# Strassen operand sums of two feed-forward layers moved from VectorE to GpSimd

## The chip, the cores and the metric

The kernel runs on one core of one Trainium2 chip. The metric is the device time of one execution in microseconds, as the median of several runs. TensorE (PE) does the matrix products, VectorE (DVE) and ScalarE (ACT) the elementwise work, GpSimd (POOL) masks and small fills. A product's result goes to a bank of PSUM, everything else lies in SBUF.

## What is computed

One layer of a hybrid decoder trunk on 1024 tokens of width 1024, in float32, cut here to what the change touches:

```python
def swiglu(h, w_gate, w_up, w_down):
    a = jnp.einsum("bld,df->blf", h, w_gate)
    b = jnp.einsum("bld,df->blf", h, w_up)
    return jnp.einsum("blf,fd->bld", jax.nn.silu(a) * b, w_down)

x = x + 0.5 * swiglu(rms_norm(x, ffn1_norm), ffn1_w_gate, ffn1_w_up, ffn1_w_down)   # D_FF = 2816
x = x + hybrid_mixer(rms_norm(x, mix_norm), ...)      # gated delta rule heads and Mamba2 heads
x = x + 0.5 * swiglu(rms_norm(x, ffn2_norm), ffn2_w_gate, ffn2_w_up, ffn2_w_down)
return rms_norm(x, final_norm)
```

## The kernel before

**Precision.** A float32 operand is split into two tiles, hi and lo. `split2` does it: ScalarE casts the operand to hi (L239), VectorE subtracts hi from the operand and so gets lo (L240). A product of weights `a` and tokens `b` is then three matmuls for each of 4 blocks of the contraction: hi by hi (L332), hi by lo (L333), lo by hi (L334), 12 in all, into a bank of 128x512. In the trace the parts are called `ah`, `al`, `bh`, `bl`.

**Strassen.** Gate and up projections multiply 2x2 blocks in seven products instead of eight. Product 1 takes `r11 + r22` of the tokens and `a11 + a22` of the weights, product 5 `r22` and `a11 + a12`, product 7 the token block (0, k + 4) plus `r22` and `a12 - a22`. The operands of the first weight tiles of gate and up are made ahead of the main loop. `b_first` and `b_second` make the token operands: TensorE transposes a block of tokens into a PSUM bank (L216), VectorE scales it by the norm's weights and adds or subtracts the other block (L279), or for product 1 adds two blocks in SBUF (L294). `a_start(n)` makes the weight operands, four or two at a time, by `a_ops`: a sum of two 128x512 pieces (L315), then the split. The table `A_START` says which: entry 2 has products 5 and 7 for gate and up (four sums), entry 3 has product 1 for gate and up (two sums).

**What stands in which order.** The code calls, in `b_second`, `between(0)` (which runs the first products through `first_products` and then `a_start` 2), then the splits of `r22`, then four operands of product 7 (k = 0 to 3), then `between(1)` (`a_start` 3), then four operands of product 1. A scheduler then sets the order of each engine's queue, and an engine works its queue strictly in that order. `gate_up_all` follows: product 6, product 5, product 7 and product 1 of the first two tiles, then the other 20 tiles one after the other in a fixed pattern. The results of the first products, of 6 and of 7 are copied out of their banks by ScalarE (L341), which frees the bank.

**Buffers.** Each of these operands is first made in a buffer of tag `q`, of which there are 4. Two of them are held by `m3`, the copies of product 3, until L400 in `gate_up_all`. So the four weight sums, four operands of product 7, two more weight sums and four token sums, 14 operands in this order, go through two buffers in turn: an operand is made when the L240 subtraction of the operand two places ahead of it has read its buffer. The banks of tag `sc`, into which the transposes write, are two as well: the transposes for k = 2 and k = 3 of product 7 write banks that L279 for k = 0 and k = 1 must have read.

Of the kernel before, what the change touches and what calls it, by code (L numbers as in the profile page):

```python
# [16 lines left out]
ALU = mybir.AluOpType  # L17
# [27 lines left out]
def kernel(  # L45
# [7 lines left out]
    V, A, G, T = nc.vector, nc.scalar, nc.gpsimd, nc.tensor  # L53
# [158 lines left out]
    def transposed(xns, k):  # L212

        pt = psum("sc")
        for i in range(4):
            T.transpose(pt[:, i * P:(i + 1) * P], xns[i][:, k * P:(k + 1) * P], ident)  # L216
        return pt
# [20 lines left out]
    def split2(hi, lo, src):  # L238
        return (A.copy(out=hi, in_=src),  # L239
                V.tensor_tensor(out=lo, in0=src, in1=hi.bitcast(F32), op=ALU.subtract))  # L240

    def split(hi, lo, src):
        return split2(hi, lo, src)[1]
# [9 lines left out]
    def b_op(H, m):  # L253
        if m not in H:
            pool, th, tl = B_TAGS[m]
            pool = pool or hbp[0]
            H[m] = (pool.tile([P, 4, 512], F32R, name=f"bh{m}", tag=th),
                    pool.tile([P, 4, 512], F32R, name=f"bl{m}", tag=tl))
        return H[m]
# [11 lines left out]
    def b_second(pool, x0, x1, wcol, H, r11, r22, between):  # L271

        def operand(m, k, f):
            t = pool.tile([P, 512], F32, name="bs", tag="q")
            f(t)
            return split2(b_op(H, m)[0][:, k], b_op(H, m)[1][:, k], t)

        def scaled(pt, kx, other, op):
            return lambda t: V.scalar_tensor_tensor(out=t, in0=pt, scalar=wcol[:, kx:kx + 1], in1=other,  # L279
                                                    op0=ALU.mult, op1=op)  # L280

        for k in range(4):
            A.mul(out=r22[:, k], in_=transposed(x1, k + 4), mul=wcol[:, k + 4:k + 5])
            p12 = transposed(x1, k)
            operand(3, k, scaled(p12, k, r22[:, k], ALU.subtract))
            operand(6, k, scaled(p12, k, r11[:, k], ALU.add))
        between(0)
        for k in range(4):
            split(b_op(H, 5)[0][:, k], b_op(H, 5)[1][:, k], r22[:, k])
        for k in range(4):  # L290
            operand(7, k, scaled(transposed(x0, k + 4), k + 4, r22[:, k], ALU.add))
        between(1)
        for k in range(4):
            last = operand(1, k, lambda t: V.tensor_tensor(out=t, in0=r11[:, k], in1=r22[:, k], op=ALU.add))  # L294
        return last

    A_GROUPS = ((3, 2, 1, 5), (4, 7, 6))
# [3 lines left out]
        nc.sync.dma_start(out=raw, in_=w.rearrange("(k p) c -> p k c", p=P)[:, :, p * 256:(p + 1) * 256])  # L301
        return raw

    def a_ops(pool, *prods):

        hi = wp.tile([P, 4, 4, P], F32R, name="ah", tag="whi")
        lo = wp.tile([P, 4, 4, P], F32R, name="al", tag="wlo")
        for i, (raw, m, ops) in enumerate(prods):
            a11, a12 = raw[:, 0:4, 0:P], raw[:, 4:8, 0:P]
            a21, a22 = raw[:, 0:4, P:2 * P], raw[:, 4:8, P:2 * P]  # L310
            v = {3: a11, 4: a22, 2: (a21, a22, ALU.add), 1: (a11, a22, ALU.add), 5: (a11, a12, ALU.add),
                 7: (a12, a22, ALU.subtract), 6: (a21, a11, ALU.subtract)}[m]
            if isinstance(v, tuple):
                t = pool.tile([P, 4, P], F32, name="as", tag="q")
                V.tensor_tensor(out=t, in0=v[0], in1=v[1], op=v[2])  # L315
                v = t
            last = split2(hi[:, i], lo[:, i], v)
            ops[m] = hi[:, i], lo[:, i]
        return last


    A_START = (((0, 2), (0, 4), (1, 2), (1, 4)), ((0, 3), (1, 3), (0, 6), (1, 6)),
               ((0, 5), (1, 5), (0, 7), (1, 7)), ((0, 1), (1, 1)))

    def a_start(pool, raws, ops, n):
        a_ops(pool, *((raws[j], m, ops[j]) for j, m in A_START[n]))

    def prod(H, bank, ops, m, first):
        (wh, wl), (bh, bl) = ops[m], H[m]
# [357 lines left out]
    with ExitStack() as c1:  # L687
        npool = NormPool(ffn_pools(c1))
        H = {}
        with tc.tile_pool(name="x1", bufs=1, side="right", reuse_waits="tile") as xp, \  # L690
# [5 lines left out]
            raws = [a_load(ffn1_w_gate[0], 0), a_load(ffn1_w_up[0], 0)]  # L696
            for b in range(4, NB):
                nc.sync.dma_start(out=xt[b], in_=x_v[:, b])
            ops = [{}, {}]
            x0, last = normalise_pairs(npool, xt, "h6")  # L700
            with tc.issue_after(last.ins), tc.issue_after(cols_in.ins):
                a_start(npool, raws, ops, 0)
            r11, r22 = (kp.tile([P, 4, 512], F32, name=f"keepx{i}") for i in range(2))
            with tc.issue_after(last_t.ins):
# [3 lines left out]
            last = b_second(npool, x0, x1, nrm[0], H, r11, r22,  # L708
                     start_rest(npool, H, ffn1_w_gate[0], ffn1_w_up[0], raws, ops))
# [100 lines left out]
    with tc.tile_pool(name="gtmp", bufs=1, side="right", reuse_waits="tile") as tp:  # L810
# [23 lines left out]
        for b in range(NB):  # L834
# [12 lines left out]
                        in1=bias.unsqueeze(1).to_broadcast([P, NB, NG]), op=ALU.add)  # L847
# [11 lines left out]
        for c in (15, 13, 11, 9, 7, 5, 3):  # L859
# [8 lines left out]
                               in1=alog.unsqueeze(1).to_broadcast([P, NB, NG]),  # L868
# [11 lines left out]
                        op=ALU.subtract)  # L880
# [19 lines left out]
    for un in range(4):  # L900
# [37 lines left out]
        for b0 in range(0, NB, 2):  # L938
# [6 lines left out]
            for name, lst, sc in (("xdt", xdts, bc2(dtn, b0)), ("xe", xes, bc2(dxe, b0))):  # L945
                t = s1.tile([P, 2, 256], F32, name=name, tag=name, bufs=4)
                last_x = V.tensor_tensor(out=t.rearrange("p i (h c) -> p i h c", h=4), in0=ptv, in1=sc,
                                         op=ALU.mult)
# [42 lines left out]
        for b0 in range(0, NB, 4):  # L991
# [33 lines left out]
            for b, py, *_ in pairs:  # L1025
                for j in range(2):
                    xv = xst[j][:, b * P:(b + 2) * P]
                    V.scalar_tensor_tensor(out=xv, in0=xv, scalar=dcol[:, 2 * un + j:2 * un + j + 1],
                                           in1=py[:, j * 256:(j + 1) * 256], op0=ALU.mult, op1=ALU.add)
# [71 lines left out]
    with ExitStack() as cg:  # L1101
        g1 = cg.enter_context(tc.tile_pool(name="gdn1", bufs=1, reuse_waits="tile"))
        g2 = cg.enter_context(tc.tile_pool(name="gdn2", bufs=2, reuse_waits="tile"))
        for h in range(GH):
# [33 lines left out]
            for half in range(2):  # L1138
# [4 lines left out]
                for i in range(4):  # L1143
# [6 lines left out]
                                in1=wend[:, hb, h:h + 1].to_broadcast([P, 4, P]), op=ALU.mult)  # L1150
# [3 lines left out]
            for b0 in range(0, NB, 2):  # L1154
# [7 lines left out]
                for i in range(2):  # L1162
# [4 lines left out]
                                in0=pg.rearrange("p (i c) -> p i c", i=2)[:, :, P:2 * P],  # L1167
                                in1=dt[:, b2], op=ALU.mult)
# [24 lines left out]
            for half in range(2):  # L1193
                pt = psum("mx")
                for i in range(4):
# [4 lines left out]
                                in1=rin[:, hb].unsqueeze(2).to_broadcast([P, 4, P]), op=ALU.mult)  # L1200
# [12 lines left out]
            for j in range(31):  # L1213
                r, n = j // 4 + 1, 31 - j
                t = ft[:, 0:r * n].rearrange("p (s l) -> p s l", l=n)
                V.tensor_tensor(out=t, in0=fx[:, 0:r, j:j + 1].to_broadcast([P, r, n]),
                                in1=fu[:, j:j + 1, j + 1:32].to_broadcast([P, r, n]), op=ALU.mult)
# [51 lines left out]
            for b in range(NB):  # L1269
                bs = slice(b * P, (b + 1) * P)  # L1270
                rr = vr[:, b]
                if st is not None:
# [4 lines left out]
                                           in1=vr[:, b], op0=ALU.mult, op1=ALU.add)  # L1277
# [8 lines left out]
                if b < NB - 1:  # L1286
# [5 lines left out]
                    else:  # L1292
                        V.scalar_tensor_tensor(out=sn, in0=st, scalar=egt[:, b, h:h + 1],
                                               in1=p3[:, 0:P], op0=ALU.mult, op1=ALU.add)
# [100 lines left out]
    raws = [a_load(ffn2_w_gate[0], 0), a_load(ffn2_w_up[0], 0)]  # L1395
    ops = [{}, {}]
# [3 lines left out]
    for b in range(NB):  # L1400
# [3 lines left out]
        if b == 5:  # L1404
            x0 = normalise(0, npool, xt2, jtag="h6")
            r11, r22 = (natp.tile([P, 4, 512], F32, name="keepx", tag=t) for t in ("nat", "zg"))
            b_first(npool, x0, nrm[2], H, r11)
    x1 = normalise(1, npool, xt2, jtag="h7")
    last = b_second(npool, x0, x1, nrm[2], H, r11, r22, start_rest(npool, H, ffn2_w_gate[0], ffn2_w_up[0], raws, ops))
    c2.close()  # L1410
    cn.close()
# [24 lines left out]
    def between():  # L1436

        with tc.issue_after(dn.last.ins):
            for b in range(4):
                V.scalar_tensor_tensor(out=xt2[b], in0=xt2[b], scalar=rows[1][:, b:b + 1], in1=rows[0],  # L1440
                                       op0=ALU.mult, op1=ALU.mult)
                nc.sync.dma_start(out=out_v[:, b], in_=xt2[b])
            for i in range(4):
                part(i, 1)
            V.tensor_scalar(out=ss[:, 4:8], in0=ss[:, 4:8], scalar1=1.0 / D, scalar2=EPS,
                            op0=ALU.mult, op1=ALU.add)
# [39 lines left out]
```

## Time and profile before

| what | value |
| --- | --- |
| median of 3 runs (lowest to highest) | 2311.04 us (2310.92 to 2312.38) |
| the profiled execution: its own time, its span | 2311.93 us, 2310.2 us |
| granted TensorE clock over the span | 0.999 |
| busy: PE, DVE, ACT, POOL | 99%, 74%, 48%, 2% |

The profile is one execution. Its span runs from the first to the last instruction; the time of the execution holds 1.7 us more. "Busy" is the share of the span in which an engine had an instruction under way. The clock is the mean of what TensorE was granted, 1 being its full speed.

### The profile page before, as it was taken

To read this page: it belongs to the slowest core of one execution; us is meant where nothing else is said; L and a number is where in the kernel's file an instruction comes from. 1 tells how busy PE (TensorE), PEld (TensorE's weight loads), DVE (VectorE), ACT (ScalarE), POOL (GpSimd) and SP (SyncE) were. 2 spreads that over 40 slices of the span, in tenths; PEclk is the share of its full clock that TensorE was granted. 3 is DMA by queue.
4 is the path that set the end of the run, shared out by engine and by line. 5 is a ranking of instruction groups with operands and counts; after the bars stand their busy time and mean duration, and the time that the engine had idled before them with its cause. 6 is when DMAs were issued, how large, how long until landed. Compare 5 with 4: busy or idle time off the path is not lost.

```text
span 2310.2 us, 31439 instructions
## 1 busy us (share of the span) xinstructions
PE 2278.0 (99%) x11766; PEld 1869.7 (81%) x11766; DVE 1701.6 (74%) x3149; ACT 1118.0 (48%) x2120; POOL 52.0 (2%) x125
## 2 busy tenths in 40 slices
PE   7999999999999999999999999999999999999998
PEld 5788888888878888887888888888878888888886
DVE  8977776767765675667778777778698777766777
ACT  7433333343467785864655456532543333334334
POOL 0000000000000000000000000000000000000000
PEclk9999999999999999999999999999999999999999
DMA  3333232574652322222333222335223333329455
GB/s 111 131 111 106 100 114 91 178 278 128 227 177 75 92 92 73 73 87 74 83 101 83 72 77 64 119 99 192 92 81 117 109 104 105 108 89 351 140 156 214
DMA packets 220956, 281.33 MB, mean 122 GB/s; under 512 B 47008, under 2 KB 153564, under 8 KB 219780
## 3 DMA queue, kind: packets, MB, share of 16 engines
q1 hardware_dynamic: 220548, 279.23, 37.2%
q8 instruction: 92, 1.51, 0.3%
q14 instruction: 60, 0.49, 0.1%
q0 software_dynamic: 256, 0.10, 0.0%
HBM read 211.55 MB, written 67.73 MB: 121 GB/s over the span
## 4 chain that ended last, share of the span: by engine, by line
PE 86%; DVE 7%; ACT 3%; DMA 2%; issue 1%; POOL 0%; SPq 0%; DVEq 0%; ACTq 0%
PE ps_pj L121 10%; PE ps_pj L122 10%; PE ps_pj L123 10%; PE ps_pj L332 6%; PE ps_pj L334 6%; PE ps_pj L333 6%; PE ps_mx L332 3%; PE ps_mx L334 3%; PE ps_mx L333 3%; PE ps_pj L553 2%; PE ps_pj L554 2%; PE ps_pj L552 2%; PE ps_oo L334 2%; PE ps_oo L332 2%; PE ps_oo L333 2%
## 5 line engine op out<-in xcount | busy, mean ns | idle before, releaser
L121 PE MATMUL ps_pj<-hhi,whi 128*128 128x512 f32 x832 | 333.9, 401 | 0.4 <-ACT gsb L826 0.4
L123 PE MATMUL ps_pj<-hhi,wlo 128*128 128x512 f32 x832 | 333.3, 401 | 0.0
L122 PE MATMUL ps_pj<-hlo,whi 128*128 128x512 f32 x832 | 332.7, 400 | 0.0
L334 PE MATMUL ps_pj<-bh,al 128*128 128x512 f32 x688 | 267.9, 389 | 0.0
L333 PE MATMUL ps_pj<-bl,ah 128*128 128x512 f32 x688 | 267.8, 389 | 0.0
L332 PE MATMUL ps_pj<-bh,ah 128*128 128x512 f32 x688 | 267.6, 390 | 0.0
L123 PEld LDWEIGHTS ps_pj<-hhi,wlo 128*128 128x128 f32 x832 | 157.1, 189 | 29.4 <-issue 0.7
L121 PEld LDWEIGHTS ps_pj<-hhi,whi 128*128 128x128 f32 x832 | 157.2, 189 | 29.0 <-ACT gsb L826 0.8
L122 PEld LDWEIGHTS ps_pj<-hlo,whi 128*128 128x128 f32 x832 | 157.0, 189 | 28.0
L239 ACT CAST ah<-wst 128x512 fp32r<-128x512 f32 x88 | 54.6, 622 | 223.1 <-PE ps_oo L333 125.3
L333 PEld LDWEIGHTS ps_pj<-bl,ah 128*128 128x128 f32 x688 | 129.2, 188 | 26.8
L334 PEld LDWEIGHTS ps_pj<-bh,al 128*128 128x128 f32 x688 | 129.1, 188 | 26.8
L332 PEld LDWEIGHTS ps_pj<-bh,ah 128*128 128x128 f32 x688 | 128.9, 188 | 26.5
L239 ACT CAST hid<-hraw 128x1024 fp32r<-128x1024 f32 (+1 forms) x84 | 82.3, 981 | 140.2 <-PE ps_oo L554 60.1
L315 DVE TENSOR_TENSOR as<-wst 128x512 f32<-128x512 f32 x220 | 145.0, 684 | 2.0 <-DMA wst<-in_ffn_w_up_dram 1.7
L240 DVE TENSOR_TENSOR al<-as,ah 128x512 fp32r<-128x512 f32 x220 | 140.9, 685 | 5.0 <-ACT ah L239 4.3
L332 PE MATMUL ps_mx<-bh,ah 128*128 128x512 f32 x352 | 138.3, 395 | 4.0 <-ACT m L341 1.4
L333 PE MATMUL ps_mx<-bl,ah 128*128 128x512 f32 x352 | 138.2, 393 | 0.5 <-DVE bl L240 0.5
L334 PE MATMUL ps_mx<-bh,al 128*128 128x512 f32 x352 | 137.5, 391 | 0.3 <-DVE al L240 0.3
L239 ACT CAST ah<-as 128x512 fp32r<-128x512 f32 x220 | 125.0, 617 | 22.6 <-DVE as L315 22.6
L240 DVE TENSOR_TENSOR hid<-hraw,hid 128x1024 fp32r<-128x1024 f32 (+1 forms) x84 | 95.0, 1131 | 31.6 <-ACT hid L239 31.0
L137 DVE TENSOR_TENSOR wlo<-wst,whi 128x1024 fp32r<-128x1024 f32 x64 | 77.5, 1218 | 48.6 <-ACT whi L136 30.5
(448 smaller groups left out, 5085.0 us busy)
## 6 DMA issues: line engine op xcount, KB each, us to landing
hraw<-hid_scr SPq DMA_DIRECT2D x70, 512.0 KB, 4.3
hid_scr<-hs SPq DMA_DIRECT2D x110, 256.0 KB, 2.3
wst<-in_ffn_w_down_dram SPq DMA_DIRECT2D x50, 512.0 KB, 4.7
wst<-in_ffn_w_gate_dram SPq DMA_DIRECT2D x22, 1024.0 KB, 5.6
wst<-in_ffn_w_up_dram SPq DMA_DIRECT2D x22, 1024.0 KB, 5.4
wst<-in_w_in_dram SPq DMA_DIRECT2D x36, 512.0 KB, 5.3
hid_scr<-sg SPq DMA_DIRECT2D x44, 256.0 KB, 2.0
keep<-in_ffn_w_down_dram SPq DMA_DIRECT2D x20, 512.0 KB, 6.4
```

Source lines behind the costliest of these rows:

```text
L121: T.matmul(o, lhsT=wh, rhs=mh, start=first, stop=False)
L122: T.matmul(o, lhsT=wh, rhs=ml, start=False, stop=False)
L123: T.matmul(o, lhsT=wl, rhs=mh, start=False, stop=last)
L137: V.tensor_tensor(out=lo[sl], in0=st[sl], in1=hi[sl].bitcast(F32), op=ALU.subtract)
L239: return (A.copy(out=hi, in_=src), V.tensor_tensor(out=lo, in0=src, in1=hi.bitcast(F32), op=ALU.subtract))
L240: V.tensor_tensor(out=lo, in0=src, in1=hi.bitcast(F32), op=ALU.subtract))
L315: V.tensor_tensor(out=t, in0=v[0], in1=v[1], op=v[2])
L332: T.matmul(bank, lhsT=wh[:, k], rhs=bh[:, k], start=a, stop=False, skip_group_check=True)
L333: T.matmul(bank, lhsT=wh[:, k], rhs=bl[:, k], start=False, stop=False, skip_group_check=True)
L334: T.matmul(bank, lhsT=wl[:, k], rhs=bh[:, k], start=False, stop=z, skip_group_check=True)
L552: T.matmul(bank, lhsT=hh, rhs=wh, start=first and k == 0, stop=False, skip_group_check=True)
L553: T.matmul(bank, lhsT=hh, rhs=wl, start=False, stop=False, skip_group_check=True)
```

## The change

Twenty sums change their engine: in each of the two feed-forward layers the four weight sums of `a_start` 2, the two of `a_start` 3, and the four token sums of product 1. What they read, where they write and who splits them stays. `G` is GpSimd, `V` VectorE.

```diff
@@ b_second @@
         for k in range(4):
-            last = operand(1, k, lambda t: V.tensor_tensor(out=t, in0=r11[:, k], in1=r22[:, k], op=ALU.add))
+            last = operand(1, k, lambda t: G.tensor_tensor(out=t, in0=r11[:, k], in1=r22[:, k], op=ALU.add))
@@ a_ops, a_start @@
-    def a_ops(pool, *prods):
+    def a_ops(pool, *prods, eng=None):
...
-                V.tensor_tensor(out=t, in0=v[0], in1=v[1], op=v[2])
+                (eng or V).tensor_tensor(out=t, in0=v[0], in1=v[1], op=v[2])
...
-        a_ops(pool, *((raws[j], m, ops[j]) for j, m in A_START[n]))
+        a_ops(pool, *((raws[j], m, ops[j]) for j, m in A_START[n]), eng=G if n > 1 else V)
```

The scheduler then orders the queues anew. First GpSimd's queue in the first feed-forward layer, behind the loads of the small columns (`as` is a weight sum, `wst` the raw weights, `bs` a token sum, `keepx0` and `keepx1` are `r11` and `r22`):

```order
 L102 DMA colst2_207<-in_ffn2_norm_dram 8x128
+L315 TENSOR_TENSOR as_559<-wst_220 128x512
+L315 TENSOR_TENSOR as_563<-wst_222 128x512
+L315 TENSOR_TENSOR as_567<-wst_220 128x512
+L315 TENSOR_TENSOR as_571<-wst_222 128x512
+L315 TENSOR_TENSOR as_625<-wst_220 128x512
+L315 TENSOR_TENSOR as_629<-wst_222 128x512
+L294 TENSOR_TENSOR bs_637<-keepx0_281,keepx1_282 128x512
+L294 TENSOR_TENSOR bs_643<-keepx0_281,keepx1_282 128x512
+L294 TENSOR_TENSOR bs_647<-keepx0_281,keepx1_282 128x512
+L294 TENSOR_TENSOR bs_651<-keepx0_281,keepx1_282 128x512
 L776 MEMSET pre_5412 128x3
```

All ten sums stand in the same order as the operands have in the code, and nothing else of GpSimd's stands among them; the second layer has ten more behind the mixer's last fill. VectorE's queue keeps the rest of that stretch as it was: the subtractions L240 and the four L279 in the order they had, without the sums between them.

Second, TensorE's queue in the first layer, in the matmuls of product 5 of the gate tile (`bh_575` and `bl_576` are the split `r22`, `ps_pj` the bank; the two groups of four transposes are those for k = 2 and k = 3 of product 7):

```order
 L333 MATMUL ps_pj<-bl_576,ah 128x512
 L334 MATMUL ps_pj<-bh_575,al 128x512
+L216 MATMUL ps_sc<-ident,xt 128x128 x4
 L332 MATMUL ps_pj<-bh_575,ah 128x512
+L216 MATMUL ps_sc<-ident,xt 128x128 x4
 L333 MATMUL ps_pj<-bl_576,ah 128x512
 L334 MATMUL ps_pj<-bh_575,al 128x512
...
 L332 MATMUL ps_pj<-bh_575,ah 128x512
 L333 MATMUL ps_pj<-bl_576,ah 128x512
-L216 MATMUL ps_sc<-ident,xt 128x128 x4
 L334 MATMUL ps_pj<-bh_575,al 128x512
-L216 MATMUL ps_sc<-ident,xt 128x128 x4
```

The transposes moved ahead: before 14 matmuls of product 5 stand in front of the first group, now 6. In the second layer they moved in the same way within product 6 of the up tile, from behind its 11th matmul to behind its 7th. Product 1 is ordered anew as well. In the first layer the matmuls of gate and up were mixed, now all 12 of gate stand ahead of the 12 of up. In the second layer 16 of the 24 stood ahead of product 7, which has 24 matmuls too, and 8 behind it; now 12 and 12.

Third, TensorE's queue in the first layer at the third pair of weight tiles (`bh4`, `bl4` are the tokens of product 4, `bh2` of product 2, `bh1` of product 1, `ps_mx_993` the bank of products 2 and 4):

```order
 L333 MATMUL ps_mx_993<-bl2_290,ah_875 128x512
 L334 MATMUL ps_mx_993<-bh2_289,al_876 128x512
-L332 MATMUL ps_mx_993<-bh4_300,ah_960 128x512
-L333 MATMUL ps_mx_993<-bl4_301,ah_960 128x512
-L334 MATMUL ps_mx_993<-bh4_300,al_961 128x512
-L332 MATMUL ps_mx_993<-bh4_300,ah_960 128x512
-L333 MATMUL ps_mx_993<-bl4_301,ah_960 128x512
-L334 MATMUL ps_mx_993<-bh4_300,al_961 128x512
-L332 MATMUL ps_mx_993<-bh4_300,ah_960 128x512
-L333 MATMUL ps_mx_993<-bl4_301,ah_960 128x512
 L332 MATMUL ps_pj_1008<-bh1_639,ah_875 128x512
 L333 MATMUL ps_pj_1008<-bl1_640,ah_875 128x512
```

Most of product 4 (8 of its 12 matmuls) moved behind products 1 and 5; it stood directly behind product 2, for whose copy out of the same bank it waits. Eight matmuls of product 4 moved behind product 5 at the tile ahead of this one too, and four in the second layer.

## Rows read from the trace of the kernel before

**Rows 1.** The page: busy time of each engine, share of the span, instructions.

```profile
PE 2278.0 (99%) x11766; PEld 1869.7 (81%) x11766; DVE 1701.6 (74%) x3149; ACT 1118.0 (48%) x2120; POOL 52.0 (2%) x125
```

**Rows 2.** TensorE's waits: line, what for, us in total, times, longest.

```profile
PE ps_mx L332 <- ACT m L341: 1.4, 2, 0.7
PE ps_sc L332 <- ACT bh L239: 1.3, 1, 1.3
...
PE ps_mx L332 <- ACT sg L378: 0.8, 1, 0.8
...
PE ps_sc L333 <- DVE bl L240: 0.5, 1, 0.5
...
PE ps_mx L334 <- DVE al L240: 0.3, 1, 0.3
```

**Rows 3.** Timeline of TensorE, first layer: start, us, instruction, [idle before].

```profile
50.99 0.39 PE L332 MATMUL ps_pj<-bh,ah 128*128 128x512 f32 x1
...
54.17 0.60 PE L216 MATMUL ps_sc<-ident,xt 128*128 128x128 f32 x4
...
62.81 0.61 PE L332 MATMUL ps_sc<-bh,ah 128*128 128x512 f32 x2
...
68.69 0.39 PE L332 MATMUL ps_pj<-bh,ah 128*128 128x512 f32 x1
...
72.39 0.50 PE L332 MATMUL ps_mx<-bh,ah 128*128 128x512 f32 x1 [0.82 <-ACT sg L378]
```

**Rows 4.** Timeline of VectorE, first layer; x2 is two like instructions in one row.

```profile
44.85 0.68 DVE L240 TENSOR_TENSOR bl<-bs,bh 128x512 fp32r<-128x512 f32 x1
45.45 0.68 DVE L240 TENSOR_TENSOR bl<-keepx,bh 128x512 fp32r<-128x512 f32 x1
46.05 0.69 DVE L240 TENSOR_TENSOR bl<-bs,bh 128x512 fp32r<-128x512 f32 x1
...
50.27 1.29 DVE L315 TENSOR_TENSOR as<-wst 128x512 f32<-128x512 f32 x2
...
52.86 1.40 DVE L279 SCALAR_TENSOR_TENSOR bs<-ps_sc,cols,keepx 128x512 f32<-128x512 f32 x2
...
57.21 0.68 DVE L240 TENSOR_TENSOR bl<-bs,bh 128x512 fp32r<-128x512 f32 x1
```

**Rows 5.** Timeline of ScalarE, first layer: a cast to hi.

```profile
57.33 0.62 ACT L239 CAST bh<-bs 128x512 fp32r<-128x512 f32 x1 [0.59 <-DVE bs L279]
```

**Rows 6.** Timelines of GpSimd and VectorE where both work.

```profile
1.19 0.29 POOL masks.py:199 TENSOR_SCALAR_AFFINE_SELECT ident<-ident 128x128 f32<-128x128 f32 x1
834.54 1.10 POOL L895 TENSOR_SCALAR_AFFINE_SELECT md<-md 128x1024 f32<-128x1024 f32 x1 [9.95 <-ACT cte L976]
1168.41 2.16 POOL L895 TENSOR_SCALAR_AFFINE_SELECT dt<-dt 128x1024 f32<-128x1024 f32 x1 [15.74 <-ACT qe L1126]
1168.34 1.28 DVE L784 SCALAR_TENSOR_TENSOR kt<-pre,cols,kt 128x1024 f32<-128x1024 f32 x1
1169.54 1.10 DVE L1216 TENSOR_TENSOR ft<-fx,fu 128x60 f32<-128x60 f32 x1
1293.36 0.22 DVE L1216 TENSOR_TENSOR ft<-fx,fu 128x60 f32<-128x60 f32 x1
```

**Rows 7.** Timelines of VectorE, TensorE and ScalarE, second layer.

```profile
1679.73 1.89 DVE L240 TENSOR_TENSOR bl<-keepx,bh 128x512 fp32r<-128x512 f32 x3
1687.19 1.40 DVE L279 SCALAR_TENSOR_TENSOR bs<-ps_sc,cols,keepx 128x512 f32<-128x512 f32 x2
1685.69 0.39 PE L332 MATMUL ps_oo<-bh,ah 128*128 128x512 f32 x1
1700.94 0.40 PE L332 MATMUL ps_pj<-bh,ah 128*128 128x512 f32 x1
1708.26 0.39 PE L332 MATMUL ps_pj<-bh,ah 128*128 128x512 f32 x1
1700.15 0.58 ACT L341 COPY m<-ps_pj 128x512 f32<-128x512 f32 x1
```

## The prediction

> **What bounds the kernel now.** The first thing to read is the page's list of busy times: TensorE is busy 99% of the span, VectorE 74%, GpSimd 2% [rows 1]. TensorE sets the end, and work taken off VectorE pays only where TensorE waits for VectorE, or for a ScalarE cast that VectorE feeds. So the second view is the list of TensorE's waits. Of those in the gate and up stage, where the twenty sums lie, five can hang on this change: 1.4 + 1.3 + 0.8 + 0.5 + 0.3 = 4.3 us [rows 2]. Were every one gone, the kernel would end 4.3 us earlier, 0.19%. A measurement of this kernel can tell about 0.2%, 4.6 us, from no change. So VectorE's relief cannot show by itself, and the question is what the move costs. For that the third view is the timeline around the sums: which operand is made when, and when TensorE needs it.
>
> **What the change removes.** Twenty sums leave VectorE. Two in a row take 1.29 us [rows 4], so one takes 0.6 us of the queue: 12 us less of VectorE's work in 2310. TensorE hardly waits for it, so this is worth at most the 4.3 us above.
>
> **What it adds: the price of one sum on GpSimd.** No row shows a sum of two tiles on GpSimd. The nearest rows are its masks: 128 elements per partition take 0.29 us, 1024 take 1.10 us [rows 6]. A mask reads one tile and writes one. A sum of 512 reads two, 1024 elements in all, so I take 1.10 us. The lower bound is a sum that reads its two inputs side by side: 0.29 + (1.10 - 0.29) x 384/896 = 0.64 us, hardly dearer than on VectorE. The upper bound counts all three streams, 1536 elements against 1024: 1.65 us. [...] No run here shows such a sum yet.
>
> **What it adds: the two engines exclude each other.** In the mixer VectorE's sum of 128x60 takes 0.22 us by itself, but 1.10 us when GpSimd's mask runs [rows 6]. The mask of 1168.41, a row that takes 2.16 us instead of 1.10, began while VectorE's operation of 1168.34 was under way, which ran on to 1169.62. So each waits until the other's whole instruction has ended, and where both have work they take turns. VectorE's sums and subtractions read two tiles from SBUF as those rows do; so I let each GpSimd sum hold up each L240, and the other way round. [...]
>
> **First layer, step by step.** Fourteen operands go through two buffers, each by three steps: make, cast (0.62 us [rows 5]), subtract (0.60 us). Before, the make and the subtraction shared one queue; now the make is in another, and its buffer comes free at the same subtraction as before. So the sums can't run ahead, and each is longer.
> - The L240 of 44.85 [rows 4] frees the first buffer at 45.5. VectorE holds until 46.05, then sum 1 runs until 47.15; the L240 of 46.05 slips to 47.15, one more goes until 48.35, sum 2 runs to 49.45, and three subtractions to 51.25. Sums 3 and 4 run from 51.25 to 53.45, their subtractions end at 54.05 and 54.70. Only then L279 for k = 0 runs: 54.70 instead of 52.86 [rows 4], 1.84 us late.
> - TensorE now has the transposes for k = 2 behind 6 matmuls of product 5, whose first starts at 50.99. One matmul is 0.227 us (14 from 50.99 to 54.17 [rows 3]), so it arrives at 52.35. They overwrite the bank that L279 for k = 0 reads until 55.36. TensorE stands some 3.0 us at a place where it did not wait before. From there to product 1 lie 62.81 - 52.35 = 10.5 us of its work, so product 1 begins near 65.9, +3.1 us.
> - The operands behind follow by the same turns. The subtraction for k = 2 comes 4.35 us behind L279 (52.86 to 57.21 [rows 4]) and ends at 59.7. Sum 5 to 60.8, k = 3 to 61.4, subtraction 5 to 62.0, sum 6 to 63.1, first token sum to 64.2, subtraction 6 to 64.8, token subtraction to 65.45, then two token sums to 67.65, two subtractions to 68.85, the fourth token sum to 69.95, its cast to 70.6, its subtraction to 71.3. Gate's product 1 needs that one and ends near 71.8; up's 12 matmuls stand behind it, until 74.5. What followed at 68.69 [rows 3] starts 5.8 us late.
> - Given back: the 0.8 us for the Silu at 72.39 [rows 2, 3] is covered by the delay, and product 4's wait for a copy, half of the 1.4, with the 0.3 behind it [rows 2], goes because products 1 and 5 now stand ahead of it: 1.8 us. First layer: 5.8 - 1.8 = +4.0 us.
>
> **Second layer.** Sums 1 and 2 come between the subtractions of 1679.73 [rows 7] and end at 1682.5, their subtractions at 1684.9, sums 3 and 4 at 1687.1, their subtractions at 1688.4. L279 starts 1.2 us late (1687.19 [rows 7]). TensorE reaches the transposes at 1685.69 + 7 x 0.227 = 1687.3 and waits until 1689.1, 1.8 us. The fourth token sum ends 15.25 us behind L279 as in the first layer (54.70 to 69.95), at 1703.65, its cast at 1704.3. The copy of product 6 stands behind that cast in ScalarE's queue (1700.15 [rows 7]) and ends at 1704.9; product 7 needs its bank. So product 7 starts 4.0 us after 1700.94, and 4 more matmuls of product 1 stand behind it (32 matmuls took from 1700.94 to 1708.26 [rows 7], 0.229 each): +4.9 us. The other half of the 1.4 us [rows 2] goes, 0.7. Second layer: +4.2 us.
>
> **The sum.** +4.0 + 4.2 = +8.2 us. The profiled execution was 2311.93 us with a span of 2310.2; it would be 2320.1 and 2318.4. It lies 0.9 above the median of 2311.04, so the median comes to **2319.2 us**. With another price of a sum the same steps give some 18 us per us: 2310.8 at 0.64, 2329 at 1.65.
>
> **Rivals.**
> - *No exclusion.* If GpSimd and VectorE run side by side here (the rows that wait have other operations than these), sums of 1.10 us still go through two buffers, and L279 starts at 52.75, no earlier than now; I find +0.6 - 1.8 = -1.2 us for the first layer, +0.9 - 0.7 = +0.2 for the second: 2310.0 us. This is the case on the other side. Against it stand the 1.10 and the 2.16 us [rows 6]. Even all waits gone would give 2306.7, at the border of what can be told, so it is "same".
> - *Short sums.* If a sum takes 0.64 us, delays and returns cancel: 2310.8 us. From about 0.65 us upward the move loses. For it speaks that 128 elements cost 0.29 us, so much of a short instruction is fixed [rows 6]; against it, that an engine that needs 0.8 us for 896 more elements of one stream would take a second stream for nothing.
> - *Long sums.* At 1.4 us, between the reading of two streams and of three: 2310.8 + 18 x 0.76 = 2324.5 us. [...]
>
> **How the numbers follow.** The forecast (exclusion, about 1.1 us) gets 0.62: two kinds of rows show the turns, and the price hangs on one assumption. Long sums 0.12, short or partly covered ones 0.16, no exclusion 0.10. The first two are slower by more than 0.2%, 0.74 in all. Short sums and no exclusion make 0.26; most of it lies within 4.6 us of 2311.0, 0.22, and 0.04 is left for a gain above it, if the new order of the later tiles removes more waits than I counted. Range: 2312 takes in the upper edge of the short sums, 2325 the long sums at 1.4 us. Outside lie no exclusion with the shortest sums, about 0.13, and sums near 1.65 us, about 0.06.
>
> **What would show it.** Right: rows of GpSimd L315 and L294 of about 1.1 us, longer where they begin under a subtraction; L240 rows of 1.2 us and more beside them; TensorE's transposes L216 with an idle time of 2 to 3 us released by VectorE's L279, in each layer; product 1 beginning about 3 us later against its layer's start and waiting several times for casts and subtractions of token sums; the stretch after product 1 without the waits for Silu and the copy. Wrong: L279 at its old place, GpSimd sums below 0.7 us, or L240 rows of 0.68 us beside a running sum. A granted clock below the 0.999 of before, behind TensorE's new idle time, would add to the sum; I count nothing for it. A wait of TensorE in the mixer that was not there before would mean that the order moved where I did not look.

## The result and the profile after

The changed kernel takes 2323.31 us (median of 6 runs, 2321.74 to 2325.08) against 2312.51 us (6 runs, 2310.92 to 2313.44): 1.0048 times as long, 95% interval 1.0035 to 1.0061, 10.8 us by the medians. The forecast was 8.2 us more, 2319.2, with a range of 2312 to 2325. Of the 4.1 us between 2319.2 and 2323.31, 1.5 lie in the kernel before, whose median stood at 2311.04 for the forecast. The profiled execution is the slowest of the six: 2325.08 us, span 2323.3, which is 13.1 us more than the span before.

The page's busy times of the changed kernel, in the form of [rows 1]:

```profile
PE 2282.1 (98%) x11766; PEld 1873.0 (81%) x11766; DVE 1704.4 (73%) x3129; ACT 1118.3 (48%) x2120; POOL 82.3 (4%) x145
```

Twenty instructions left VectorE (3149 to 3129), yet its busy time did not fall: 1701.6 before, 1704.4 now. At 0.6 us each, 12 us should have gone. They came back as time in which its other instructions are under way longer. That one line already suggests that the second engine brought no overlap; what holds those instructions, it does not say.

The list of TensorE's waits of the changed kernel, in the form of [rows 2]; the rows that are new or grew in the gate and up stage:

```profile
PE ps_sc L216 <- DVE bs L279: 5.8, 2, 3.7
...
PE ps_sc L333 <- DVE bl L240: 2.6, 3, 1.3
PE ps_sc L332 <- ACT bh L239: 2.3, 1, 2.3
...
PE ps_pj L332 <- ACT sg L454: 1.1, 1, 1.1
```

The forecast wait at the transposes is there in both layers, 3.7 and 2.1 us (3.0 and 1.8 were forecast), and the waits in product 1 for subtractions and a cast of token sums. The waits for a copy (1.4) and for Silu (0.8) of [rows 2] are gone; a new one for a Silu of a later tile takes back 1.1. Outside that stage two rows changed. The down projection's wait at L553 grew from 1.5 to 2.2 us, and there is a new wait in the mixer, at 650.66:

```profile
PE ps_sc L216 <- ACT xtb L186: 0.7, 1, 0.7
```

The prediction had named a new wait in the mixer as a sign that the order moved where it did not look. Where this one comes from is not shown.

The timeline of GpSimd in the first layer, and of VectorE beside it:

```profile
46.59 4.67 POOL L315 TENSOR_TENSOR as<-wst 128x512 f32<-128x512 f32 x2 [40.56 <-DVE bl L240]
51.88 1.28 POOL L315 TENSOR_TENSOR as<-wst 128x512 f32<-128x512 f32 x1 [0.63 <-DVE al L240]
53.80 1.26 POOL L315 TENSOR_TENSOR as<-wst 128x512 f32<-128x512 f32 x1 [0.63 <-DVE al L240]
61.55 2.99 POOL L315 TENSOR_TENSOR as<-wst 128x512 f32<-128x512 f32 x2 [6.50 <-DVE bl L240]
65.18 1.29 POOL L294 TENSOR_TENSOR bs<-keepx,keepx 128x512 f32<-128x512 f32 x1 [0.63 <-DVE al L240]
```

```profile
47.57 1.28 DVE L240 TENSOR_TENSOR bl<-keepx,bh 128x512 fp32r<-128x512 f32 x2
50.69 5.74 DVE L240 TENSOR_TENSOR al<-as,ah 128x512 fp32r<-128x512 f32 x4 [1.84 <-ACT ah L239]
56.35 1.40 DVE L279 SCALAR_TENSOR_TENSOR bs<-ps_sc,cols,keepx 128x512 f32<-128x512 f32 x2
...
67.15 6.43 DVE L240 TENSOR_TENSOR bl<-bs,bh 128x512 fp32r<-128x512 f32 x4
```

A sum takes 1.26 to 1.29 us where nothing holds it, and GpSimd stands 0.63 us between two sums, until the subtraction that frees the next buffer has ended. Four subtractions of token sums take 6.43 us. L279 comes at 56.35 instead of 52.86 [rows 4]. Of these 3.5 us, 0.9 are no work of the change: the load of small columns at the start landed 0.9 us later in this execution (TensorE's second wait there is 3.7 us instead of 2.8).

TensorE's timeline at the same place (first layer up to 76.95, then second layer):

```profile
57.15 1.11 PE L216 MATMUL ps_sc<-ident,xt 128*128 128x128 f32 x4 [3.74 <-DVE bs L279]
...
70.37 0.39 PE L332 MATMUL ps_sc<-bh,ah 128*128 128x512 f32 x1
...
72.81 0.50 PE L333 MATMUL ps_sc<-bl,ah 128*128 128x512 f32 x1 [0.69 <-DVE bl L240]
...
76.95 0.39 PE L332 MATMUL ps_pj<-bh,ah 128*128 128x512 f32 x1
...
1695.33 0.65 PE L216 MATMUL ps_sc<-ident,xt 128*128 128x128 f32 x4 [2.06 <-DVE bs L279]
...
1705.33 0.50 PE L332 MATMUL ps_sc<-bh,ah 128*128 128x512 f32 x1 [2.31 <-ACT bh L239]
...
1721.70 0.39 PE L332 MATMUL ps_pj<-bh,ah 128*128 128x512 f32 x1
```

The row of 76.95 is that of 68.69 [rows 3]: 8.3 us later, 7.4 without the 0.9 of the start (5.8 forecast). Behind the waits for Silu and copies the delay is 6.9 us, 6.0 without the start (4.0 forecast). The row of 1721.70 is that of 1708.26 [rows 7], 13.4 us later. The first transposes of that layer, before and now:

```profile
1666.56 0.66 PE L216 MATMUL ps_sc<-ident,xt 128*128 128x128 f32 x4 [0.34 <-ACT xt L186]
1672.39 0.66 PE L216 MATMUL ps_sc<-ident,xt 128*128 128x128 f32 x4 [0.32 <-ACT xt L186]
```

They were 5.8 us late already, so the second layer adds 7.6 up to there (4.9 forecast) and 6.8 behind the wait that is gone (4.2 forecast). That they are 5.8 late and not 6.9 is no gain of the change. In the mixer the new wait costs 0.7, but in the profiled execution of before eight matmuls at 846 to 849 us ran at the lower clock, at 0.43 us each, and in that of the changed kernel they did not, which is 1.4 us.

The table of windows of the changed kernel shows one thing that the sum left out, the clock (columns: stretch and its length, busy time and instructions of five engines, granted clock of TensorE, share of the DMA engines, GB/s):

```profile
57.20:62.70 5.50, 5.50 (x17) 4.60 (x18) 4.67 (x7) 3.47 (x6) 1.15 (x1) 0.50 0.00 0
63.00:70.00 7.00, 7.00 (x32) 5.75 (x32) 5.61 (x4) 2.97 (x5) 5.11 (x5) 1.00 0.81 250
1695.30:1697.00 1.70, 1.67 (x12) 1.50 (x13) 1.57 (x3) 1.24 (x2) 0.00 (x0) 1.00 0.00 0
...
1709.10:1714.70 5.60, 5.60 (x13) 4.37 (x14) 5.44 (x8) 1.59 (x3) 1.23 (x1) 0.50 0.03 10
```

Behind the 3.74 us without work TensorE's granted clock is 0.50 for some 5.5 us, and again in the second layer behind the waits of 2.31, 1.29 and 0.67 us. A matmul then takes 0.43 us instead of 0.227 from one start to the next.

### The profile page after: what moved, and what is told of

Same layout as the page of the kernel before. It is cut to its first block, busy times and chain, and to the rows that moved or that the text cites. A ratio compares the mean times of both kernels' runs of the same rounds, so it can differ in the third digit from the quotient of the medians.

```text
span 2323.3 us, 31460 instructions
## 1 busy us (share of the span) xinstructions
PE 2282.1 (98%) x11766; PEld 1873.0 (81%) x11766; DVE 1704.4 (73%) x3129; ACT 1118.3 (48%) x2120; POOL 82.3 (4%) x145
## 4 chain that ended last, share of the span: by engine, by line
PE 83%; DVE 8%; ACT 3%; DMA 3%; issue 2%; POOL 1%; SPq 0%; DVEq 0%; ACTq 0%; POOLq 0%
PE ps_pj L121 10%; PE ps_pj L122 10%; PE ps_pj L123 10%; PE ps_pj L332 6%; PE ps_pj L334 6%; PE ps_pj L333 6%; PE ps_mx L332 3%; PE ps_mx L334 3%; PE ps_mx L333 3%; PE ps_pj L553 2%; DMA wst<-in_ffn_w_down_dram 2%; PE ps_pj L554 2%; PE ps_pj L552 2%; PE ps_oo L332 1%; PE ps_oo L334 1%
## 5 line engine op out<-in xcount | busy, mean ns | idle before, releaser
L240 DVE TENSOR_TENSOR al<-as,ah 128x512 fp32r<-128x512 f32 x220 | 147.0, 711 | 10.8 <-ACT ah L239 9.6
L315 DVE TENSOR_TENSOR as<-wst 128x512 f32<-128x512 f32 x208 | 137.1, 682 | 2.0 <-DMA wst<-in_ffn_w_up_dram 1.9
L240 DVE TENSOR_TENSOR hid<-hraw,hid 128x1024 fp32r<-128x1024 f32 (+1 forms) x84 | 94.9, 1130 | 31.4 <-ACT hid L239 30.9
```

Source lines behind the costliest of these rows:

```text
L315: (eng or V).tensor_tensor(out=t, in0=v[0], in1=v[1], op=v[2])
```

## The experiments

All of them are compared with the kernel before on the same chip. Two theories came out of the result. **Chain**: the cost is the length of the chain of operands through two buffers. **Order**: the cost is that TensorE's transposes were moved ahead to a place where they wait. A third, **exclusion**, that GpSimd's sums cost time wherever VectorE works, was set against them in the second set of runs.

**One half of the change at a time.** `e1_weights_only` takes the token sums back, `e2_tokens_only` the weight sums:

```diff
 # e1_weights_only, b_second
-            last = operand(1, k, lambda t: G.tensor_tensor(out=t, in0=r11[:, k], in1=r22[:, k], op=ALU.add))
+            last = operand(1, k, lambda t: V.tensor_tensor(out=t, in0=r11[:, k], in1=r22[:, k], op=ALU.add))
 # e2_tokens_only, a_start
-        a_ops(pool, *((raws[j], m, ops[j]) for j, m in A_START[n]), eng=G if n > 1 else V)
+        a_ops(pool, *((raws[j], m, ops[j]) for j, m in A_START[n]))
```

> Only the twelve weight sums on GpSimd, the eight token sums back on VectorE. The order of TensorE's queue is that of the changed kernel in the first layer: the transposes of product 7 stand behind 6 matmuls of product 5. Theory chain (the cost is the chain of operands through two buffers, which grows by what a GpSimd sum takes more than a VectorE sum): of the 10 sums per layer 6 stay, and the four token sums fall back to 0.6 us each; of the 11 us lost some 7 remain, 2318 to 2320 us. Rival order (the cost is TensorE's wait at the transposes that were moved ahead, with the lower clock behind it): the same wait of 3.7 and 2.1 us and nearly the whole loss, 2321 to 2324 us.

> Only the eight token sums on GpSimd, the weight sums back on VectorE. The transposes stand where they stood before the change. Theory chain: four longer sums per layer at the chain's end, where TensorE waits for them: 2 us per layer, less what was slack, 2314 to 2317 us. Rival order: TensorE does not wait at the transposes, no loss that can be told, 2310 to 2313 us.

Measured: 2318.41 us for the weight sums alone, 1.0029 (1.0018 to 1.0039), 6.6 us by the medians; 2315.52 for the token sums alone, 1.0018 (1.0009 to 1.0028), 3.7 us. Together 10.2 of the change's 10.8 us. The first run has the same waits at the transposes as the change, the same row word for word (5.8 us, twice, longest 3.7), and loses 4 us less; the second has none of them and still loses. Chain is right on both, order on neither.

**The sums twice as long.** `e4_twice` makes each GpSimd sum two times in a row:

```diff
-                (eng or V).tensor_tensor(out=t, in0=v[0], in1=v[1], op=v[2])
+                for _ in range(2 if eng is G else 1):
+                    (eng or V).tensor_tensor(out=t, in0=v[0], in1=v[1], op=v[2])
 # the token sums in the same way
```

> Each of the twenty GpSimd sums is made twice in a row, into the same buffer (the second is superfluous; the result is the same). The scheduler then puts TensorE's transposes back to some 10 matmuls behind the start of product 5 in the first layer and to their place of before in the second. Theory chain: 10 sums per layer are 1.27 us longer each; by the slope of the prediction, 18 us per us of a sum, 23 us on top of the 11 us: 2340 to 2350 us. Rival order: with the transposes further back the loss shrinks or stays, 2315 to 2325 us.

Measured: 2344.14 us, 1.0137 (1.0120 to 1.0153), 32.3 us over the kernel before, 21.5 more than the change's 10.8: the chain's range. For 1.27 us more per sum that is 17 us per us; the prediction's steps gave 18. The granted clock over the span is lower too, 0.991 to 0.993 against 0.996 to 0.997 in the change, and 0.83 from 50 to 100 us and 0.89 from 1690 to 1750 us in the profiled execution. So a part of these 17 may belong to the clock; no run parts the two.

**The transposes moved back.** `e8_late_transposes` writes products 6 and 5 ahead of the last two operands of product 7:

```diff
+            if n == 2:
+                six = [open_bank(H, st, "c22", 6, None, ("pj", "oo")[j]) for j, st in enumerate(ops)]
+                five = [prod(H, st["c12"], st, 5, False) for st in ops]
+                return five[0][3] if w_gate.name.startswith("ffn1") else six[1][3]
...
         for k in range(4):
-            operand(7, k, scaled(transposed(x0, k + 4), k + 4, r22[:, k], ALU.add))
+            late = between(2) if k == 2 else late if k else None
+            with tc.issue_after(late.ins) if k > 1 else nullcontext():
+                pt = transposed(x0, k + 4)
+            operand(7, k, scaled(pt, k + 4, r22[:, k], ALU.add))
```

The rest of the edit takes the same calls out of `gate_up_all`.

> All twenty sums on GpSimd as in the change, but products 6 and 5 of the first two tiles are written ahead of the last two operands of product 7, so that their transposes stand behind all matmuls of product 5. Theory chain: TensorE no longer waits at the transposes, and waits for the later operands instead; the end of the chain is the same, 2320 to 2324 us. Rival order: without the wait at the transposes the loss goes, 2311 to 2316 us.

Measured: 2328.75 us, 1.0071 (1.0056 to 1.0086), 17 us. Neither number came. The two layers have to be read apart, on TensorE's timeline of this run:

```profile
56.47 1.16 PE L216 MATMUL ps_sc<-ident,xt 128*128 128x128 f32 x8
...
76.21 0.39 PE L336 MATMUL ps_pj<-bh,ah 128*128 128x512 f32 x1
...
1700.65 1.03 PE L216 MATMUL ps_sc<-ident,xt 128*128 128x128 f32 x8
...
1709.00 0.80 PE L336 MATMUL ps_sc<-bh,ah 128*128 128x512 f32 x1 [7.32 <-ACT bh L239]
```

In the first layer the transposes wait for nothing (no bracket at 56.47), and the row that stood at 68.69 before still begins at 76.21, 7.5 us late, as in the change. So there the wait at the transposes moved the idle time but did not make it: TensorE waits within product 1 instead, for the operands of the token sums (0.41, 1.30 and 0.92 us), and the end of the chain sets when product 1 ends. (This layer too has a stretch at the lower clock, 0.53 from 70.0 to 73.6, where a matmul takes 0.43 us from one start to the next.) In the second layer the edit overshot. VectorE's L279 for k = 2 waited 3.0 us for the transposes behind all of product 5, everything behind it in the chain slipped, and TensorE waited 7.3 us for a cast.

**The price by itself.** `e9_bench` leaves out the layer and runs stretches of GpSimd's and VectorE's instructions alone and together.

> A program by itself that leaves out the whole layer and copies x to the output: sums of two 128x512 tiles on GpSimd alone, of 128x128 and 128x1024 too, copies on GpSimd, VectorE subtractions alone, and both engines at once with VectorE's input from two SBUF tiles, from PSUM and one SBUF tile, from one SBUF tile, and with a ScalarE cast ahead of each subtraction. Theory (two reading engines exclude each other, a sum alone is 1.27 us): 1.27 us a GpSimd sum alone and 0.60 a subtraction alone; together with two SBUF inputs the stretch is the sum of both, 12 x 0.60 + 4 x 1.27 = 12.3 us; with PSUM or one input VectorE's rows stay as alone. Rival (both slow down because they share bandwidth, or nothing is shared): the stretch is below 9 us, with rows between, or both at their own pace.

The timelines of GpSimd and VectorE in that run (L88, L91, L94: sums of 512, 128 and 1024 elements alone; L100: subtractions alone; L103 and L105: both; L108 and L110: VectorE with one input from PSUM and one from SBUF, and the sums; L113 and L115: VectorE with a single input, from SBUF, and the sums):

```profile
19.09 7.36 POOL L88 TENSOR_TENSOR go<-c,d 128x512 f32<-128x512 f32 x6 [1.86 <-ACT d L78]
27.23 1.69 POOL L91 TENSOR_TENSOR go<-c,d 128x128 f32<-128x128 f32 x4 [0.78 <-ACT d L78]
29.70 9.23 POOL L94 TENSOR_TENSOR go<-c,d 128x1024 f32<-128x1024 f32 x4 [0.78 <-ACT d L78]
...
47.19 6.51 POOL L105 TENSOR_TENSOR go<-c,d 128x512 f32<-128x512 f32 x4 [5.30 <-ACT d L78]
59.57 4.94 POOL L110 TENSOR_TENSOR go<-c,d 128x512 f32<-128x512 f32 x4 [5.88 <-ACT d L78]
68.05 5.51 POOL L115 TENSOR_TENSOR go<-c,d 128x512 f32<-128x512 f32 x4 [3.54 <-ACT d L78]
```

```profile
42.37 3.70 DVE L100 TENSOR_TENSOR vo<-a,b 128x512 f32<-128x512 f32 x6 [26.04 <-ACT b L76]
46.88 11.57 DVE L103 TENSOR_TENSOR vo<-a,b 128x512 f32<-128x512 f32 x12 [0.81 <-ACT b L76]
59.27 7.99 DVE L108 SCALAR_TENSOR_TENSOR vo<-pt,cols,b 128x512 f32<-128x512 f32 x12 [0.82 <-ACT b L76]
67.75 8.86 DVE L113 TENSOR_SCALAR vo<-b,cols 128x512 f32<-128x512 f32 x12 [0.48 <-ACT b L76]
```

This is one execution. A sum alone begins every 1.22 us ((7.36 - 1.27) / 5) and lasts 1.27 by the groups of instructions; VectorE's subtraction alone 0.60 ((3.70 - 0.68) / 5). Twelve subtractions beside four sums take 11.57 us. One after the other they would take 12 x 0.60 + 4 x 1.22 = 12.1, side by side 7.3. So nearly nothing overlaps. With one input from PSUM VectorE needs 7.99 us for twelve, which begin every 0.66 us ((7.99 - 0.74) / 11), and the four sums take 4.94 and begin every 1.22 us as alone: no exclusion there. With a single input, from SBUF, the expectation failed: it said that VectorE's rows stay as alone. They begin every 0.40 us alone and take 0.47; the four that stood beside sums took 1.48 each, and the four sums 5.51 instead of 4.94. So the exclusion holds for this instruction too. In the stretch with a ScalarE cast ahead of each subtraction it holds as well: its eight subtractions beside four sums took 8.85 us, where eight of 0.60 us take 4.9, and the longest took 1.75 us instead of 0.68.

**The sums out of the chain.** `e3_w_inplace` writes the sums of products 5 and 7 over raw weights that nobody reads any more; `e6_all_inplace` writes the token sums over r11 as well; `e7_all_inplace_v` is the same with VectorE making all of them:

```diff
 # e3 and e6
-                t = pool.tile([P, 4, P], F32, name="as", tag="q")
+                t = {5: a21, 7: a12}[m] if m in (5, 7) and eng else pool.tile([P, 4, P], F32, name="as", tag="q")
 # e6; with V in place of G here and in a_start: e7
-            last = operand(1, k, lambda t: G.tensor_tensor(out=t, in0=r11[:, k], in1=r22[:, k], op=ALU.add))
+            G.tensor_tensor(out=r11[:, k], in0=r11[:, k], in1=r22[:, k], op=ALU.add)
+            last = split2(b_op(H, 1)[0][:, k], b_op(H, 1)[1][:, k], r11[:, k])
```

> As the change, but the eight weight sums of products 5 and 7 are written over pieces of the raw weights that nobody needs any more, instead of into one of the two buffers. So 10 operands per layer go through the two buffers, not 14. Theory chain: L279 for k = 0 of product 7 no longer stands behind four GpSimd sums and comes 2 to 3 us earlier than in the kernel before; the six sums at the end of the chain still cost some 3 us per layer: together 2309 to 2316 us. Rival exclusion (the cost is that GpSimd's twenty sums of 1.27 us hold VectorE up, wherever they stand): 2320 us or more.

> As the change, with the weight sums of products 5 and 7 over dead pieces of the raw weights and the four token sums over r11, so that of GpSimd's sums only the two weight sums of product 1 go through the two buffers. Theory chain: no TensorE wait hangs on GpSimd any more, 2307 to 2312 us. Rival exclusion: the same twenty sums hold VectorE up, 2318 us or more.

> The same places for the sums as in the run before it, but all twenty made by VectorE. Theory chain: TensorE was bound by its own work, so taking the operands out of the two buffers is worth at most the 4.3 us of waits, 2307 to 2311 us, and GpSimd makes no difference of its own to it, within 2 us of that run. Rival exclusion: some 8 us faster than that run.

Measured: e3 2324.21 us, 1.0057 (1.0042 to 1.0072); e6 2318.81, 1.0031 (1.0019 to 1.0044); e7 2307.42, 0.9985 (0.9976 to 0.9995). Chain by itself fell: with eight of GpSimd's sums out of the chain e3 loses as much as the change, with sixteen out of it e6 still loses 7 us, while the same places with VectorE gain 4 us. By the medians they are 12.7 and 7.3 us over the kernel before, and 4.1 us under it. The edits of e6 and e7 differ in the engine alone, and that makes 11.4 us between them; the scheduler orders the queues anew in each, but of TensorE's 11766 matmuls only 96 stand in another place. Their timelines in the first layer show where. VectorE, GpSimd and TensorE of e6:

```profile
29.07 1.27 DVE L112 TENSOR_SCALAR rstd<-ssv 128x4 int32<-128x4 int32 x1
...
30.86 1.26 DVE L116 SCALAR_TENSOR_TENSOR rs_t<-rstd,ssv 128x4 f32<-128x4 f32 x1
...
27.36 8.28 POOL L316 TENSOR_TENSOR wst<-wst 128x512 f32<-128x512 f32 x4 [21.34 <-DVE ssv L166]
...
38.55 0.66 PE L216 MATMUL ps_sc<-ident,xt 128*128 128x128 f32 x4 [4.11 <-ACT xt L186]
```

VectorE and TensorE of e7:

```profile
28.25 0.16 DVE L112 TENSOR_SCALAR rstd<-ssv 128x4 int32<-128x4 int32 x1
...
36.28 0.66 PE L216 MATMUL ps_sc<-ident,xt 128*128 128x128 f32 x4 [0.34 <-ACT xt L186]
```

Freed from the buffers, the four weight sums ran as soon as they could, into the normalisation of the second half of the tokens. Of the ten 0.16 us instructions of VectorE's there, the four that met a sum took 1.23 to 1.27 us, about as long as a whole sum, and TensorE waited 4.1 us for the normalised tokens; its transposes began at 38.55, 2.3 us later than in e7.

**The same sums held back.** In `e11_inplace_held` a small GpSimd copy from the last block of r22 stands ahead of the four weight sums:

```diff
+        gate[:] = [G.tensor_copy(out=pool.tile([P, 1], F32, name="gt"), in_=r22[:, 3, 0:1])]
         between(0)
...
+                with tc.issue_after(gate[0].ins) if eng is G else nullcontext():
```

> As the run with all sums in place on GpSimd, but the four weight sums of products 5 and 7 (and the sums behind them in GpSimd's queue) wait for the last block of r22, so that they no longer fall into the normalisation of the second half of the tokens. Theory (exclusion costs where VectorE feeds TensorE): TensorE's wait of 4.1 us at the transposes of the normalised tokens in the first layer goes, and what the sums hold up behind r22 remains: 2309 to 2316 us. Rival (the loss of that run is a fixed cost of twenty GpSimd sums): 2317 us or more.

Measured: 2319.95 us, 1.0037 (1.0023 to 1.0051). TensorE's 4.1 us at the normalised tokens went, as expected (0.3 us are left), but the time did not: it is 9.6 us over the kernel before, in the rival's range (2317 or more). TensorE's queue has the same order as in e6. VectorE and TensorE of this run:

```profile
47.15 5.22 DVE L241 TENSOR_TENSOR bl<-bs,bh 128x512 fp32r<-128x512 f32 x3 [0.38 <-ACT bh L240]
...
58.41 0.66 PE L216 MATMUL ps_sc<-ident,xt 128*128 128x128 f32 x4 [1.94 <-DVE bs L280]
```

Three subtractions took 5.22 us instead of 1.9, and TensorE waited 5.3 us in three places for L280 (the old L279) instead. The loss moved with the sums. The rival's fixed cost of twenty GpSimd sums does not fit all runs either, since the same twenty cost 7.3 us in e6, 9.6 here, 10.8 in the change and 12.7 in e3. That the expectation was too low because TensorE needs VectorE's results in every stretch of this stage is argued, not shown.

**VectorE as slow as GpSimd.** `e10_v_twice` is the kernel before with VectorE making each of the twenty sums twice, 1.2 us of its queue, and GpSimd not used:

```diff
-                V.tensor_tensor(out=t, in0=v[0], in1=v[1], op=v[2])
+                for _ in range(times):
+                    V.tensor_tensor(out=t, in0=v[0], in1=v[1], op=v[2])
 # times=2 from A_START entry 2 on; the token sums in the same way
```

> The kernel before, with VectorE making each of the twenty sums twice in a row into the same buffer (the second is superfluous): 1.2 us of VectorE's queue for a sum, as long as a GpSimd sum, and no GpSimd at all. Theory (a GpSimd sum excludes VectorE, so a second engine brings no overlap, and what counts is that each sum takes 1.27 instead of 0.6 us): the loss is that of the change, 10 sums x 2 layers x 0.6 us with the rest of the chain unchanged, 2320 to 2326 us. Rival (GpSimd does run beside VectorE, and the loss comes from somewhere else, such as hand-over between the engines): clearly slower than the change, 2328 us or more, or far below it, under 2317 us.

Measured: 2324.34 us, 1.0060 (1.0045 to 1.0075). By the medians that is 14.0 us, within the range expected, and the interval overlaps that of the change, 1.0048 (1.0035 to 1.0061). In VectorE's timeline of this run L279 comes 3.0 us late. Its first row here is that of 44.85 in [rows 4], 0.6 us late from the start, so 2.4 us are the sums' (four times 0.6); in the change it was 2.6, without the 0.9 of the start:

```profile
45.45 0.68 DVE L240 TENSOR_TENSOR bl<-bs,bh 128x512 fp32r<-128x512 f32 x1
...
52.07 2.49 DVE L316 TENSOR_TENSOR as<-wst 128x512 f32<-128x512 f32 x4
...
55.86 1.40 DVE L279 SCALAR_TENSOR_TENSOR bs<-ps_sc,cols,keepx 128x512 f32<-128x512 f32 x2
```

TensorE does not wait at the transposes here. It waits within product 1, for casts of token sums:

```profile
PE ps_sc L333 <- ACT bh L239: 8.7, 2, 5.7
```

The loss is no smaller for that, which speaks for the length of the chain once more, and not for the order. So moving the sums to GpSimd had the effect of making VectorE do each of them twice. Beside VectorE's subtractions GpSimd is here no second engine (11.57 us for the bench's twelve and four, 12.1 one after the other), only a slower one (1.27 us a sum, not 0.6).

## Why the prediction was right

- **What bounds the kernel.** That VectorE's relief is worth at most 4.3 us agrees with e7, which takes sixteen sums out of the buffers without any exclusion: the five waits of [rows 2] are gone from its list, and it gains 4.1 us by the medians, 0.15% by the ratio. But VectorE still makes all sums there. No run relieved VectorE and changed nothing else, so the bound itself was not tried.
- **The price of a sum** was the term that was too small: 1.10 us was taken, 1.27 measured in the bench and in the change. By the prediction's slope of 18 us per us the 0.17 us make 3.1 us, and 8.2 becomes 11.3, beside 10.8 measured; the slope was 17 in e4. That this one term fills the gap by itself is luck: by that slope it makes about 1.5 us in each layer, while in the profiled execution the layers came out 2.0 and 2.6 us above their forecasts, and in the second some of that is the clock (below). To count a sum as two streams at the mask's price was too low at every size: it gives 0.41, 1.10 and 2.03 us for 128, 512 and 1024 elements, and the bench shows 0.46, 1.27 and 2.34, which is 2.1 ns per element and some 0.19 us fixed, while the masks of [rows 6] are 0.9 ns per element.
- **Exclusion** held: in the bench (11.57 us where side by side would be 7.3), in e6's 0.16 against 1.27 us, and in the L240 rows of the change (four in 6.43 us, where four of 0.60 us take 2.5). e10 agrees with it without showing it. The first rival (2310.0) is refuted by the same rows. Its premise, that the length of the sums in the chain costs nothing much as long as nothing excludes, was not tried: no run here has GpSimd's sums without VectorE's inputs in SBUF.
- **L279 late by 1.84 and 1.2 us** came out as 2.6 in the first layer and 1.5 in the second (1694.53, less 5.83, against 1687.19). In the first there are two reasons: the longer sums, and the first sum, which did not take turns. It was released at 46.59 and its partner began at 49.97, while three subtractions ran at their usual pace. The same is seen for the first sum of e6, which was released at 27.36 and ended only near 30.3, as the L112 that it held up did (30.34), while two subtractions ran at their usual pace. In the second layer, and in the bench, turns were taken at once. What made the difference is open.
- **TensorE's wait at the transposes** was forecast well, but it was not what the first layer lost, as e8 and e10 show. The forecast's sum is not touched by this, since it followed the chain to the last token sum. Product 1 itself began 6.7 us late, without the 0.9 of the start, and not 3.1 (70.37 against 62.81): the slow clock behind the wait (0.50 from 57.20 to 62.70) held TensorE back further. In return it waited only once in product 1, 0.69 us.
- **Given back**: 2.5 us were forecast, 1.8 of them in the first layer, and the waits for Silu and copies did go; the new wait for a later tile's Silu took 1.1 us back, and the first layer kept 1.4 (8.3 against 6.9).
- **The clock** was counted at nothing. Thirteen matmuls took 5.7 us instead of 3.0 from 1709.04 on, 2.7 us, and the first layer has a stretch as long. In the first layer none of that is seen to reach the end. The chain lost nothing by the slower transposes: its subtraction for k = 2 came 4.37 us behind L279 (60.72 against 56.35), as before (4.35). TensorE still had to wait for the chain at 72.81, and the chain's last subtraction ended at 73.58 (67.15 + 6.43), just before the matmul that reads it:

```profile
73.64 0.50 PE L333 MATMUL ps_sc<-bl,ah 128*128 128x512 f32 x1
```

In the second layer the chain was done first. ScalarE's copy frees product 7's bank, and product 7 begins later; then the first matmul behind gate's twelve of product 7, now and before:

```profile
1710.89 0.58 ACT L341 COPY m<-ps_pj 128x512 f32<-128x512 f32 x1
1712.19 0.63 PE L332 MATMUL ps_pj<-bh,ah 128*128 128x512 f32 x1
1716.26 0.39 PE L332 MATMUL ps_oo<-bh,ah 128*128 128x512 f32 x1
1703.73 0.39 PE L332 MATMUL ps_oo<-bh,ah 128*128 128x512 f32 x1
```

Product 7 began 0.7 us behind the copy, and its first twelve matmuls took 4.07 us instead of 2.79 (1700.94 to 1703.73). The two together are an estimate of what reaches the end: some 2 of the 2.7 us. No run has the waits without the lower clock, so it stays an estimate.

The spans' 13.1 us are 2.3 more than the medians differ (10.8), because the profiled execution of the changed kernel lies 1.8 us above its median and that of before 0.6 below its own; 0.9 of it is the late load at the start.

## What to carry to other kernels

Before work goes to an engine that idles, ask whether it can run beside the engine that it relieves: here a GpSimd sum and a VectorE instruction with both inputs in SBUF took turns, whole instruction by whole instruction (four sums and twelve subtractions in 11.57 us, 12.1 one after the other), apart from the first sum in the first layer of the change and of e6. So did the bench's one with a single input, from SBUF (1.48 us instead of 0.47), while the one with an input from PSUM ran beside the sum (one every 0.66 us, and a sum every 1.22 us as alone). So 0.6 us of VectorE's work became 1.27 us in which VectorE stands. Where operands pass through few buffers, a chain's length counts, not the load of an engine; writing a sum over an operand that nobody reads any more took the chain apart and, with VectorE, was the only version with a lower time than the kernel before (2307.42 us, 0.9985, with an interval that ends at 0.9995). A wait that shows in the trace is not the loss by itself: take it away, as in e8 and e10, and see whether the end moves.

## What had not been expected of the hardware

A VectorE instruction of four elements per partition, 0.16 us by itself (e7), took 1.23 to 1.27 us where it met one of GpSimd's sums (e6), about eight times as long, while the bench's subtraction of 512 elements took up to 1.75 us instead of 0.68. The bench's instruction with a single input, from SBUF, was held as well (1.48 us instead of 0.47), the one with an input from PSUM was not (twelve in 7.99 us, one every 0.66). And TensorE's clock fell to 0.50 behind a stretch without work of 3.74 us, and behind waits of 2.31, 1.29 and 0.67 us in the second layer, but not behind the single wait of 2.06 us at 1695.33, where the next matmuls kept their 0.23 us.
